# The last two blocks of both output projections join the feed-forward chain as a group

## The chip, the cores and the metric

The kernel runs on one core of a Trainium2 chip. TensorE (PE) multiplies, VectorE (DVE), ScalarE (ACT) and GpSimd (POOL) do the elementwise work, and SyncE (SP) and POOL issue the loads used here. The metric is the device time of one execution in microseconds; lower is better.

## The reference

A decoder trunk of two layers runs over 256 tokens of width 2048 in float32. Each layer normalises, projects, attends (layer A with compressed, selected and windowed keys, layer B with dilated windows; both also to 256 memory tokens), projects back and adds to the residual, and then runs a SwiGLU feed-forward network of inner width 5632. What this case touches is the end of each attention part and the start of each feed-forward network:

```python
o = jnp.concatenate([o_nsa, o_mem], axis=-1) @ w_out      # A: 2048 -> 2048, B: 1024 -> 2048
h = h + o
n = rms_norm(h, norm_ffn)
h = h + (jax.nn.silu(n @ w_gate) * (n @ w_up)) @ w_down   # 2048 -> 5632 -> 2048
```

## The kernel before, in words

**Numbers.** Every float32 operand is split into a high part (a copy in a rounded format, on ACT, L83) and a low part (the rest, a subtraction on DVE, L84). A block product is then three matmuls of 128 x 128 by 128 x 512: high by high, low by high, high by low (`mm3`, L92 to L94, or `hi_lo`, L102, which keeps the third ones for the end of a chunk). Activations stand still in PE, weights stream through. The 256 tokens are two halves of 128.

**Chunks.** `load_w` (L129) loads 512 KB of weights on SP's queue into one of four `raw` buffers and splits them into `whi` and `wlo`, three buffers each. One chunk feeds 12 matmuls.

**Four pairs by seven products.** Gate and up are two 512-wide column blocks, the tokens two halves. For a pair of input blocks (k, k+1) the eight block products of this 2 x 2 by 2 x 2 problem are got from seven products of sums. `Group.steps` has them as s0 to s6: each loads or sums quarters of the weights (1 MB, four pairs at once; tile `q`), splits them into `qhi` and `qlo` (128 x 2048, two buffers each), and does 12 matmuls. s1 and s2 begin with a DVE add on the quarter that the product before has just used; after each of them POOL issues a load that accumulates another quarter onto a used one. s3 uses the first of these, s5 the second. Some results are copied or subtracted between the four PSUM banks of a group. The remaining input blocks of the group are plain chunks (`plain`), one per input block, for all four banks.

The activations for this (`Paired`) are the token halves of each pair and four sums of them, `xhi` and `xlo`: a pair's turn (`turn`, L329) is four PE transposes, two ACT copies into `xf`, a split, four DVE sums of 128 x 128, and a second split. An input block that isn't in a pair has a plain turn: four transposes, two ACT copies and two DVE steps (L86, L87).

**The chain.** `run_groups` goes through the feed-forward groups: eleven gate/up blocks and, after four, four and three of them, two down-projection blocks each. While the chunks of one group run, the seven products of the next one are put between them; `spacing` says how many chunks go ahead of each. Side work (turns) is put in by ticks of three matmuls. The first gate/up block isn't in this form: it is a group of 16 plain chunks (`gu_0`), because nothing before it could carry its seven products. The buffers of the chain (pool `q`) and of its hidden activations (pool `h`) are opened after the pools of the attention part are closed.

**The output projection.** `project_out` works in four blocks of 512 columns. The first two run together as far as attention output is ready (`ready`), then each is finished; after each block the sum is added to the residual `h` (L363), its squares are summed on ACT (L255), and its two turns are put among the next block's matmuls. Blocks three and four are two more calls of `gemm`. Then the norm's factor is made (`finish_rstd`, L245 to L250), and the chain begins.

**Order.** PE's order is as written. The other engines' instructions, SP's loads among them, are ordered by a list scheduler by priority and expected readiness, and then run in that order; `urgent` raises the priority.

## Time and profile before

| what | value |
|---|---|
| median of 3 runs | 2003.47 us (2002.95 to 2003.87) |
| profiled execution | 2003.28 us, its span 2001.5 us |
| PE busy | 1990.3 us, 9315 matmuls, mean granted clock 0.998 |
| DVE busy | 1610.9 us |
| ACT busy | 1241.8 us |
| POOL busy | 66.8 us |
| DMA | 465.75 MB, mean 233 GB/s |

The span goes from the first to the last instruction of the profile. Busy is the time in which an engine worked on an instruction; matmuls are pipelined, so one that lasts 0.39 us still lets the next begin 0.23 us after it. An engine that isn't the bottleneck may stand idle at no cost.

### The profile page before, as it was taken

To read this page: it belongs to the slowest core of one execution; us is meant where nothing else is said; L and a number is where in the kernel's file an instruction comes from. 1 tells how busy PE (TensorE), PEld (TensorE's weight loads), DVE (VectorE), ACT (ScalarE), POOL (GpSimd) and SP (SyncE) were. 2 spreads that over 40 slices of the span, in tenths; PEclk is the share of its full clock that TensorE was granted. 3 is DMA by queue.
4 is the path that set the end of the run, shared out by engine and by line. 5 is a ranking of instruction groups with operands and counts; after the bars stand their busy time and mean duration, and the time that the engine had idled before them with its cause. 6 is when DMAs were issued, how large, how long until landed. Compare 5 with 4: busy or idle time off the path is not lost.

```text
span 2001.5 us, 25392 instructions
## 1 busy us (share of the span) xinstructions
PE 1990.3 (99%) x9315; PEld 1656.8 (83%) x9315; DVE 1610.9 (80%) x2006; ACT 1241.8 (62%) x1561; POOL 66.8 (3%) x96
## 2 busy tenths in 40 slices
PE   9999999999999999999999999999999999999998
PEld 7898888888888888888888888888888888888886
DVE  6767798768888888888887777877888788888886
ACT  7756576656665566656665655656665666655664
POOL 0000000000000000000000000000000000000000
PEclk9999999999999999999999999999999999999999
DMA  9867734587887878878785755497878878788784
GB/s 306 278 204 232 234 113 127 178 261 226 270 285 230 247 238 276 280 229 244 241 273 168 234 168 158 140 304 215 282 240 249 252 257 279 234 243 263 256 257 135
DMA packets 105405, 465.75 MB, mean 233 GB/s; under 512 B 12224, under 2 KB 12608, under 8 KB 83392
## 3 DMA queue, kind: packets, MB, share of 16 engines
q1 hardware_dynamic: 94896, 395.51, 55.2%
q0 software_dynamic: 9952, 67.77, 18.2%
q8 instruction: 73, 1.20, 0.2%
q10 hardware_dynamic: 432, 0.84, 0.1%
q14 instruction: 52, 0.43, 0.1%
HBM read 459.88 MB, written 4.19 MB: 232 GB/s over the span
## 4 chain that ended last, share of the span: by engine, by line
PE 98%; DVE 1%; issue 0%; DMA 0%; ACT 0%; SPq 0%; POOLq 0%; POOL 0%; DVEq 0%; ACTq 0%
PE mm L102 81%; PE mm L93 4%; PE mm L94 4%; PE mm L92 4%; PE aux L344 1%; PE aux L263 1%; PE aux L93 1%; PE aux L94 1%; PE aux L92 1%; PE aux L378 0%; PE cmp L669 0%; PE cmp L668 0%; DMA raw<-in_a_w_mem_kv_dram 0%; DVE xlo L84 0%; DVE wlo L84 0%
## 5 line engine op out<-in xcount | busy, mean ns | idle before, releaser
L84 DVE TENSOR_TENSOR qlo<-q,qhi 128x2048 fp32r<-128x2048 f32 (+1 forms) x224 | 497.9, 2224 | 152.6 <-ACT qhi L83 151.9
L83 ACT ACTIVATE whi<-raw 128x1024 fp32r<-128x1024 f32 (+1 forms) x408 | 424.6, 1043 | 314.6 <-PE mm L102 258.3
L83 ACT ACTIVATE qhi<-q 128x2048 fp32r<-128x2048 f32 (+1 forms) x224 | 417.6, 1865 | 237.5 <-PE mm L102 149.9
L84 DVE TENSOR_TENSOR wlo<-raw,whi 128x1024 fp32r<-128x1024 f32 (+1 forms) x408 | 488.6, 1201 | 94.1 <-ACT whi L83 85.9
L102 PE MATMUL mm<-whi,xhi 128*128 128x512 f32 (+1 forms) x1016 | 391.5, 387 | 0.0
L102 PE MATMUL mm<-whi,xlo 128*128 128x512 f32 (+1 forms) x1016 | 390.8, 386 | 0.0
L102 PE MATMUL mm<-wlo,xhi 128*128 128x512 f32 (+1 forms) x1016 | 273.1, 386 | 0.0
L102 PEld LDWEIGHTS mm<-whi,xlo 128*128 128x128 f32 x1016 | 191.0, 188 | 36.3
L102 PEld LDWEIGHTS mm<-whi,xhi 128*128 128x128 f32 x1016 | 190.9, 188 | 36.3
L102 PE MATMUL mm<-qhi,xhi 128*128 128x512 f32 x560 | 218.7, 391 | 0.0
L102 PE MATMUL mm<-qhi,xlo 128*128 128x512 f32 x560 | 217.9, 389 | 0.0
L102 PEld LDWEIGHTS mm<-wlo,xhi 128*128 128x128 f32 x1016 | 186.7, 188 | 36.4
L87 DVE SCALAR_TENSOR_TENSOR wlo<-raw,gains,whi 128x512 fp32r<-128x512 f32 x160 | 114.5, 747 | 50.7 <-ACT whi L86 46.0
L86 ACT ACTIVATE whi<-raw,gains 128x512 fp32r<-128x512 f32 x160 | 107.8, 717 | 69.8 <-PE mm L102 35.3
L102 PE MATMUL mm<-qlo,xhi 128*128 128x512 f32 x560 | 149.7, 389 | 0.0
L102 PEld LDWEIGHTS mm<-qlo,xhi 128*128 128x128 f32 x560 | 105.1, 188 | 22.0
L102 PEld LDWEIGHTS mm<-qhi,xhi 128*128 128x128 f32 x560 | 105.2, 188 | 21.4
L102 PEld LDWEIGHTS mm<-qhi,xlo 128*128 128x128 f32 x560 | 105.2, 188 | 21.4
L102 PE MATMUL mm<-qhi,hThi 128*128 128x512 f32 x308 | 120.6, 392 | 0.0
L102 PE MATMUL mm<-qhi,hTlo 128*128 128x512 f32 x308 | 119.9, 389 | 0.0
L102 PE MATMUL mm<-whi,hThi 128*128 128x512 f32 x296 | 115.3, 390 | 0.0
L102 PE MATMUL mm<-whi,hTlo 128*128 128x512 f32 x296 | 115.3, 389 | 0.0
(307 smaller groups left out, 2872.5 us busy)
## 6 DMA issues: line engine op xcount, KB each, us to landing
q<-in_a_gu_q_dram SPq DMA_DIRECT2D x40, 1024.0 KB, 6.4
raw<-in_a_gu_s_dram SPq DMA_DIRECT2D x80, 512.0 KB, 7.3
q<-in_b_gu_q_dram SPq DMA_DIRECT2D x40, 1024.0 KB, 6.5
raw<-in_b_gu_s_dram SPq DMA_DIRECT2D x80, 512.0 KB, 7.4
raw<-in_a_dn_s_dram SPq DMA_DIRECT2D x44, 512.0 KB, 6.4
raw<-in_b_dn_s_dram SPq DMA_DIRECT2D x44, 512.0 KB, 6.3
q<-in_a_gu_q_dram POOLq DMA_DIRECT2D x20, 1024.0 KB, 9.8
q<-in_b_gu_q_dram POOLq DMA_DIRECT2D x20, 1024.0 KB, 9.8
```

What stands on the lines that cost most here:

```text
L83: nc.scalar.activation(hi, src, AF.Copy)
L84: nc.vector.tensor_sub(lo, src, hi.bitcast(F32))
L86: nc.scalar.activation(hi, src, AF.Copy, scale=gain)
L87: nc.vector.scalar_tensor_tensor(lo, src, gain, hi.bitcast(F32), op0=ALU.mult, op1=ALU.subtract)
L92: nc.tensor.matmul(o, l[0], r[0], start=start, stop=False, skip_group_check=more)
L93: nc.tensor.matmul(o, l[1], r[0], start=False, stop=False, skip_group_check=more)
L94: nc.tensor.matmul(o, l[0], r[1], start=False, stop=stop, skip_group_check=more)
L102: nc.tensor.matmul(*args, skip_group_check=True, **kw)
L263: nc.tensor.transpose(ps[:, i * P:(i + 1) * P], s, ident)
L344: nc.tensor.transpose(ps[:, i * P:(i + 1) * P], tok[tt][:, i * P:(i + 1) * P], ident)
```

## The change

The third and fourth block of both output projections become one group, `Lead`, at the head of the chain. It has 16 (A) or 8 (B) plain chunks, of which the last three run bank by bank: after each bank's last product DVE adds it to the residual and ACT sums the squares, and after the second and the fourth bank the block's two turns are put into the side work, 4 and 7 ticks later. The seven products of the first gate/up block stand between these chunks by `LEADS`; in layer B only s0 to s4, and s5 and s6 (`own`) go between the next group's first chunks. The first gate/up block takes the form of the others: four pairs by seven products, and eight plain chunks. Side work left at the end of `Lead` is carried on (`leave`).

For this the attention output gets a pool of its own (`po`) that lives until `Lead` is done; pool `q` is opened on the other side of the memory before `Lead` begins, pool `h` after it. Within the chain the pair turns use the three `hb` buffers instead of `xf`. The weights are laid out anew: blocks three and four of `w_out` as chunks of one input block by 1024 columns.

```diff
+TICKS1 = (3, 5)
+LTICKS = (4, 7)
+LEADS = {16: (5, 3, 3, 3, 2, 0, 0), 8: (5, 1, 1, 1, 0)}
...
+        def more(self):
+            self.steps[self.done:] = sorted(self.steps[self.done:] + [(self.now + t, f) for t, f in deferred], key=lambda s: s[0])
+            deferred.clear()
+
+        def leave(self):
+            deferred.extend((t - self.now, f) for t, f in self.steps[self.done:])
+            self.done = len(self.steps)
...
-            f = fpool.tile([P, 1, 4, P], F32, tag="xf", name="xf", bufs=xf_bufs[0])
+            if fpool is fq:
+                f = fq.tile([P, 512], F32, tag="hb", name="xf", bufs=3).rearrange("p (q s t) -> p q s t", q=1, s=4)
+            else:
+                f = fpool.tile([P, 1, 4, P], F32, tag="xf", name="xf", bufs=xf_bufs[0])
...
     def project_out(name, nk, ready, gi):
...
-            residual_block(g[i].ps, i, ssq, op)
-        for nb in range(2, 4):
-            ps = gemm(ob[nb], osx, 512, nk)
-            residual_block(ps, nb, ssq, op, (3, 5) if nb == 2 else (3, 3), nb == 3)
-        return op, finish_rstd(ssq, 4)
+            residual_block(g[i].ps, i, ssq, op, TICKS1 if i else (3, 5), i == 1)
+        return op, ssq
...
+    class Lead(Group):
+        def __init__(self, xs, rest, op, ssq, done):
+            super().__init__(None, None, rest, done)
+            self.xs, self.x_op, self.ssq = xs, op, ssq
+            self.carry = True
+
+        def plain(self, c, side):
+            if c == 0:
+                self.begin()
+            n = len(self.rest)
+            if c < n - 3:
+                ws = load_w(self.rest[c], 512)
+                hi_lo([(self.bank[b], self.xs[c](b % 2), ws[b // 2]) for b in range(4)], side, c == 0)
+            elif c == n - 3:
+                ws = [load_w(self.rest[i], 512) for i in range(c, n)]
+                for b in range(4):
+                    for i, w in enumerate(ws):
+                        mm3(self.bank[b], self.xs[c + i](b % 2), w[b // 2], False, i == 2, True)
+                        side.tick()
+                    nb, tt = 2 + b // 2, b % 2
+                    hb = h[:, tt, nb * 512:(nb + 1) * 512]
+                    nc.vector.tensor_add(hb, self.bank[b], hb)
+                    square_sum(self.ssq[:, tt, nb:nb + 1], hb)
+                    if tt:
+                        deferred.extend(at([urgent(lambda nb=nb, k2=k2: self.x_op.turn(nb, k2, False)) for k2 in range(2)], *LTICKS))
+                        side.more()
...
     def run_groups(groups):
...
+            while own:
+                g.plain(c, side)
+                c += 1
+                own.pop(0)()
             if nxt is not None and nxt.q is not None:
...
-                for ahead, s in zip(spacing(n, nxt.tight), nxt.steps(side)):
-                    for _ in range(ahead):
+                nxt.side = side
+                ss = nxt.steps()
+                spaces = LEADS[n] if g.carry else spacing(n - c, nxt.tight)
+                for ahead, s in zip(spaces, ss):
+                    for _ in range(min(ahead, n - c)):
                         g.plain(c, side)
                         c += 1
                     if c == n and g.done is not None:
-                        side.flush()
+                        if not g.carry:
+                            side.flush()
                         g.done(g)
                         g.done = None
                     s()
+                own = ss[len(spaces):]
...
+        def out_done(g):
+            nonlocal f_r, fh
+            f_r = finish_rstd(ssq, 4)
+            keep.close()
+            fh = phase.enter_context(tc.tile_pool(name="h" + pre, bufs=1))
+
+        wo = a[pre + "_w_out_s"]
+        groups = [Lead(osx, [wo[k] for k in range(wo.shape[0])], op, ssq, out_done)]
...
-                if b == 0:
-                    groups.append(Group(op, None, [a[pre + "_gu_0"][k] for k in range(KT)], done))
-                else:
-                    groups.append(Group(op, [gq[b - 1, i] for i in range(4)], [gs[b - 1, c] for c in range(KT - 2 * NPX)], done))
+                groups.append(Group(op, [gq[b, i] for i in range(4)], [gs[b, c] for c in range(KT - 2 * NPX)], done))
...
     def open_ffn(name):
-        nonlocal fh, fq, fpool, work
+        nonlocal fq, fpool, work
         rota("aux")
-        fh = phase.enter_context(tc.tile_pool(name="h" + name, bufs=1))
-        work = fpool = fq = phase.enter_context(tc.tile_pool(name="q" + name, bufs=1))
+        work = fpool = fq = phase.enter_context(tc.tile_pool(name="q" + name, bufs=1, side="right"))
```

## Rows read from the trace of the kernel before

**Rows 1.** The page's totals and its row of the granted clock in 40 slices.

```profile
PE 1990.3 (99%) x9315; PEld 1656.8 (83%) x9315; DVE 1610.9 (80%) x2006; ACT 1241.8 (62%) x1561; POOL 66.8 (3%) x96
...
PEclk9999999999999999999999999999999999999999
```

**Rows 2.** Waits of PE: engine, line, releaser, us in total, times, longest.

```profile
PE aux L507 <- DVE warm L504: 1.2, 1, 1.2
PE mm L93 <- DVE olo L84: 0.6, 2, 0.3
PE mm L92 <- ACT ohi L83: 0.4, 1, 0.4
```

**Rows 3.** The chain of waits, three stretches: start us, us, what.

```profile
366.68 0.23 PE mm L92
...
415.13 52.38 PE mm L102 x231
...
563.18 0.87 PE aux L344 x8
```

**Rows 4.** Busy by stretch: length, PE, PEld, DVE, ACT, POOL, clock, DMA share, GB/s.

```profile
1281.50:1302.50 21.00, 20.93 (x102) 17.10 (x101) 20.11 (x38) 17.65 (x35) 0.00 (x0) 1.00 0.48 152
...
1374.60:1416.30 41.70, 41.70 (x190) 34.59 (x189) 36.52 (x34) 28.20 (x31) 1.73 (x2) 1.00 0.82 254
```

**Rows 5.** PE in order of time: start us, us, line, operation, tiles.

```profile
1281.19 0.60 PE L329 MATMUL aux<-ident,h 128*128 128x128 f32 x4
1281.54 0.48 PE L92 MATMUL mm<-whi,obhi 128*128 128x512 f32 x1
...
1307.67 1.03 PE L263 MATMUL aux<-ident,h 128*128 128x128 f32 x8
```

**Rows 6.** DVE in order of time, where the old first block began.

```profile
1309.09 0.88 DVE L87 SCALAR_TENSOR_TENSOR xlo<-aux,gains,xhi 128x256 fp32r<-128x256 f32 x2 [0.63 <-ACT xhi L86]
...
1315.19 2.29 DVE L84 TENSOR_TENSOR qlo<-q,qhi 128x2048 fp32r<-128x2048 f32 x1 [3.30 <-ACT qhi L83]
1317.40 2.35 DVE L84 TENSOR_TENSOR wlo<-raw,whi 128x1024 fp32r<-128x1024 f32 x2
```

**Rows 7.** DVE in order of time: the pair turns of layers A and B.

```profile
370.60 0.68 DVE L84 TENSOR_TENSOR xlo<-xf,xhi 128x512 fp32r<-128x512 f32 x1
...
1282.69 0.69 DVE L84 TENSOR_TENSOR xlo<-xf,xhi 128x512 fp32r<-128x512 f32 x1 [0.61 <-ACT xhi L83]
...
1288.13 1.29 DVE L84 TENSOR_TENSOR xlo<-xf,xhi 128x512 fp32r<-128x512 f32 x2
```

**Rows 8.** DVE's groups from 1281.5 to 1302.5: count | busy us, mean ns.

```profile
L84 DVE TENSOR_TENSOR wlo<-raw,whi 128x1024 fp32r<-128x1024 f32 x7 | 8.5, 1214 | 0.0
L84 DVE TENSOR_TENSOR xlo<-xf,xhi 128x512 fp32r<-128x512 f32 x8 | 5.4, 685 | 0.6 <-ACT xhi L83 0.6
...
L87 DVE SCALAR_TENSOR_TENSOR xlo<-aux,gains,xhi 128x256 fp32r<-128x256 f32 x4 | 1.8, 473 | 0.0
L315 DVE TENSOR_TENSOR xf<-xf 128x128 f32<-128x128 f32 x4 | 1.2, 290 | 0.1
```

**Rows 9.** SP's issues in order of time, layer B.

```profile
1293.65 11.22 SPq L129 DMA_DIRECT2D raw<-in_b_gu_dram  x6
1305.82 0.33 SPq L907 DMA_DIRECT2D q<-in_b_gu_q_dram  x1
```

**Rows 10.** PE: the last product that reads layer B's attention output.

```profile
1305.40 0.39 PE L94 MATMUL mm<-wlo,obhi 128*128 128x512 f32 x1
```

**Rows 11.** ACT: the first split of layer B's first quarter.

```profile
1313.24 1.92 ACT L83 ACTIVATE qhi<-q 128x2048 fp32r<-128x2048 f32 x1 [2.76 <-DMA q<-in_b_gu_q_dram]
```

**Rows 12.** Waits of SP's queue: us in total, times, longest.

```profile
SPq L129 <- DVE wlo L84: 1041.6, 374, 8.2
```

**Rows 13.** DMA issues: count, KB each, median us to landing.

```profile
q<-in_b_gu_q_dram SPq DMA_DIRECT2D x40, 1024.0 KB, 6.5
```

**Rows 14.** DVE in order of time: a head's turn in a steady group.

```profile
566.33 1.28 DVE L84 TENSOR_TENSOR hTlo<-aux,hThi 128x512 fp32r<-128x512 f32 x2
```

More of the change, by code (lines that the diff above doesn't have):

```diff
@@ L54, in decoder_trunk @@
     small.tile([P, PADW], F32, name="padw", bufs=1)
+    right = ctx.enter_context(tc.tile_pool(name="right", bufs=1, side="right"))
+    right.tile([P, 64], F32, name="padr")
+    keep = ctx.enter_context(ExitStack())
     phase = ctx.enter_context(ExitStack())
@@ L225, in decoder_trunk @@
     const.tile([P, 32], F32, name="padc")
+    po = keep.enter_context(tc.tile_pool(name="po", bufs=1))
     rota("b3", "aux", "b3")
@@ L500, in o_pair @@
     def o_pair():
-        return pair(lambda i: pa.tile([P, 2, T], F32R, tag=("ohi", "olo")[i], name=("ohi", "olo")[i], bufs=8))
+        return pair(lambda i: po.tile([P, 2, T], F32R, tag=("ohi", "olo")[i], name=("ohi", "olo")[i], bufs=8))
     warm = work.tile([P, 512], BF16, tag="rope2", name="warm")
@@ L924, in keep, with steps @@
             return t
-        def steps(self, side):
+        def steps(self):
             def s0():
@@ L930, in s0 @@
                 self.new(1)
-                self.product(1, 1, self.qa, side, True)
+                self.product(1, 1, self.qa, self.side, True)
                 with tc.high_priority(offset=URGENT):
@@ L938, in s1 @@
                 self.new(2)
-                self.product(2, 7, self.qa, side, True)
+                self.product(2, 7, self.qa, self.side, True)
                 nc.gpsimd.dma_start(self.qb, self.q[2], accum_op=ALU.add)
@@ L945, in s2 @@
                 nc.vector.tensor_add(self.qa, self.qa, self.qc)
-                self.product(1, 5, self.qa, side)
+                self.product(1, 5, self.qa, self.side)
                 nc.gpsimd.dma_start(self.qa, self.q[3], accum_op=ALU.add)
@@ L952, in s3 @@
             def s3():
-                self.product(1, 4, self.qb, side)
+                self.product(1, 4, self.qb, self.side)
                 with tc.high_priority(offset=URGENT):
@@ L959, in s4 @@
             def s4():
-                self.product(2, 6, self.qc, side)
+                self.product(2, 6, self.qc, self.side)
             def s5():
                 self.qb = self.load(3)
-                self.product(1, 3, self.qa, side)
+                self.product(1, 3, self.qa, self.side)
             def s6():
-                self.product(0, 2, self.qb, side)
+                self.product(0, 2, self.qb, self.side)
             return [s0, s1, s2, s3, s4, s5, s6]
@@ L1001, in run_groups @@
             g.buf = ("abc", "cab", "bca")[i % 3]
+        own = []
         for i, g in enumerate(groups):
-            side = take()
+            side = g.side = take()
             n = len(g.rest)
@@ L1021, in run_groups @@
                 c += 1
+            if g.carry:
+                side.leave()
             side.flush()
@@ L1024, in run_groups, with ffn @@
                 g.done(g)
-    def ffn(pre, op, f_r, last):
+    def ffn(pre, op, ssq, last):
         gq, gs = a[pre + "_gu_q"], a[pre + "_gu_s"]
-        groups = []
+        f_r = None
+        def out_done(g):
[5 more added lines that the diff above has]
+        groups = [Lead(osx, [wo[k] for k in range(wo.shape[0])], op, ssq, out_done)]
         for pi, (b0, b1) in enumerate(PORTIONS):
@@ L1080, in __init__, with steps @@
             self.hop = hop
-        def steps(self, side):
+        def steps(self):
             self.op = self.hop()
-            return super().steps(side)
+            return super().steps()
     class Tail(Lazy):
@@ L1128, in decoder_trunk @@
     phase.close()
+    po = keep.enter_context(tc.tile_pool(name="pob", bufs=1))
     rota("b3", "b4", "b3", "aux")
@@ L1164, in ob_slot @@
     def ob_slot():
-        t = pair(lambda i: pc.tile([P, 2, T], F32R, tag=("obhi", "oblo")[i], name=("obhi", "oblo")[i], bufs=4))
+        t = pair(lambda i: po.tile([P, 2, T], F32R, tag=("obhi", "oblo")[i], name=("obhi", "oblo")[i], bufs=4))
         osx.extend(cols((t[0][:, i, :], t[1][:, i, :])) for i in range(2))
@@ L1231, in decoder_trunk @@
     xf_bufs[0] = 3
-    fx, f_r = project_out("b_w_out", 8, 3, 6)
+    fx, f_ssq = project_out("b_w_out", 8, 3, 6)
     stack.close()
     phase.close()
-    open_ffn("fb")
+    open_ffn("b")
     gfin = None
@@ L1355, in _layout @@
     g["a_w_mem_kv"] = _blocks(np, i["a_w_mem_kv"][0])
-    g["a_w_out"] = _blocks(np, i["a_w_out"][0], order=[12, 13, 14, 15] + list(range(12)))
+    for n, order in (("a_w_out", [12, 13, 14, 15] + list(range(12))), ("b_w_out", [0, 4, 1, 5, 2, 6, 3, 7])):
+        w = _blocks(np, i[n][0], order=order, ck=1)
+        g[n] = _blocks(np, i[n][0][:, :1024], order=order)
+        g[n + "_s"] = np.ascontiguousarray(np.concatenate([w[2], w[3]], 2))
     g["w_kv_shared"] = _blocks(np, i["w_kv_shared"])
@@ L1360, in _layout @@
     g["b_w_mem_kv"] = _blocks(np, i["b_w_mem_kv"][0])
-    g["b_w_out"] = _blocks(np, i["b_w_out"][0], order=[0, 4, 1, 5, 2, 6, 3, 7])
     for pre in "ab":
         gate, up, wd = i[pre + "_w_gate"][0], i[pre + "_w_up"][0], i[pre + "_w_down"][0]
-        q, r, first = _pairs(np, gate, up, NFB, NPX)
-        g[pre + "_gu_0"] = first
-        g[pre + "_gu_q"], g[pre + "_gu_s"] = q[1:], r[1:]
+        g[pre + "_gu_q"], g[pre + "_gu_s"] = _pairs(np, gate, up, NFB, NPX)
         for pi, (b0, b1) in enumerate(PORTIONS):
```

18 lines of the change are left out of this document (9 added, 9 removed).

## The prediction

> **What bounds the kernel now.** I read the page's totals first: TensorE (PE) is busy for 1990.3 of the 2001.5 us span, at a granted clock of 9 tenths or more (the top digit) in every slice [rows 1]. A busy PE can still be a PE that waits, so the waits of PE come next: all waits together are 2.2 us, the longest of them 1.2 us and at the start-up multiplication [rows 2]. The chain of waits then gives the price of one product: 231 products in a row take 52.38 us, 226.75 ns each [rows 3]. So the kernel is a queue of products, and time goes only where products go or where a new wait comes. The next limit is VectorE (DVE): in a steady gate/up group it is busy for 36.52 of 41.70 us, ScalarE (ACT) for 28.20; in the middle of layer B's output projection DVE is busy for 20.11 of 21.00 us and PE still does not stop [rows 4]. That stretch is where the change puts new DVE work.
>
> **What is removed.** Per layer the old first gate/up block is 16 chunks of 12 products, 192. The new one is four pairs by seven products (7 x 4 x 3 = 84) and 8 chunks (96), 180. The two output blocks keep their number (192 in layer A, 96 in B), and so do the transposes, 0.87 us for eight [rows 3], 0.44 for four. So 12 products a layer go, 24 in all: 24 x 226.75 ns = 5.44 us. PE does not wait in the old stages, so nothing beyond that can be won; 5.44 is the upper end of the gain.
>
> The Trainium skill ("TensorE: Matmul & The Clock Gate", Back-to-back issue gap) gives about 131 ns per matmul of 512 columns in a stream of weight loads and matmuls, and 216 ns for an isolated one. By the first the removal would be worth 3.1 us at most, by the second 5.2; rows 3 have 226.75 ns, so the trace contradicts the first, and I give it no chance.
>
> **What is added, at no cost.** Per layer seven quarter-sums must be split on ACT and DVE, with two DVE adds and two subtractions, and two accumulating loads come on POOL's queue (2 MB more traffic). Eight chunk splits go. In layer A the new chain step (group Lead) has 276 products, 62.6 us; the DVE work due in it is some 49 us by the durations below, so PE hides it. DMA moves 14.7 MB there (234 GB/s) and 10.5 MB in layer B's 40.8 us (257 GB/s), about the 254 GB/s that a steady group carries without a wait of PE [rows 4]. The moves of pools and the new weight layout change no instruction count. In layer B two of the seven products move into the next group, which has then 6 chunks for the next block's seven: 27.8 us of DVE work in 35.4 us, hidden.
>
> **What is added, at a cost: layer B.** I count from L = 1281.54, the first product after the second block's transposes [rows 5]; it becomes Lead's first. PE's program after L is: five chunks (13.6 us) and two batches of transposes (0.9), so the first quarter-sum product, s0, is due at L+14.5. Then come the last three chunks, s1, s2, s3 and s4 without a chunk between them, with four batches of transposes; s4 ends at L+38.0, and the third of its products that reads the low part begins at L+37.1.
>
> *DVE by that deadline.* Rows overlap by about 0.08 us (2.29 us long, the next 2.21 later [rows 6]), so I count 2.20 for a quarter-sum split or add, 1.13 for a chunk split, 0.6 for a 512-wide step, 0.21 for a 128-wide sum, 0.40 for a 256-wide split [rows 6, 8]. Due: four pair turns, 8 x 0.6 + 16 x 0.21 = 8.2; chunks 3 to 8, 6.8; five splits and two adds, 15.4; two subtractions, 1.2; four residual adds, 2.4; four plain turns, 8 x 0.40 = 3.2; the norm, 0.3. Sum 37.5. The turns begin at 1282.69 [rows 7], L+1.15, so DVE ends at L+38.65 if it never idles: 1.5 us late. If the last turn and the norm slip behind the split, 0.5.
>
> *The first quarter's load.* The new block's buffers lie where the attention's pools lay. In the trace layer B's first quarter is issued 0.4 us after the last product that reads attention output began, and six chunk loads of the same block went ahead of it [rows 9, 10], so I read it as waiting for those pools to be given up. After the change attention output lives elsewhere, and the last use of the old pools is the first block's pair turn: transposed at 1281.19, split on DVE by 1289.4 [rows 5, 7], and perhaps by 1288, since the second block's turn no longer stands between its steps: L+6.5 to L+7.9. From issue to ACT's split took 7.4 us, ACT waiting [rows 9, 11]; then 1.92 for the split: L+15.8 to L+17.2, where PE wants it at L+14.5. With the median landing of 6.5 instead of 7.4 [rows 13] it is L+14.9. PE waits 0.4 to 2.7 us here. This wait and the DVE lateness are the same time seen twice (DVE works on while PE stands), so the larger counts.
>
> *Transposes through one bank.* The last two blocks' transposes go through one PSUM bank, three ticks (9 products, 2.04 us) apart. Where DVE has little to do, two batches end at 1308.70 and the first one's bank is free at 1309.97, 1.7 us after its own batch (0.43 earlier) [rows 5, 6]; in a loaded group it is 3.56 us (564.05 to 567.61) [rows 3, 14]. Three such gaps a layer cost between 0 and 3 x 1.5 = 4.6 us.
>
> I take 1.8 us for layer B (bounds 0.5 and 5: DVE's 1.5, the nearest row being its stretch at 20.11 of 21.00, and a little idleness). In layer A Lead's first product is the one at 366.68 and the first block's turn ends at 371.28 [rows 3, 7]; 7.4 and 1.92 us later, at 13.9 after Lead's start, s0's split is ready, just before 14.5, and DVE has 13 us to spare. Only the bank's gaps count, 0.4 (bounds 0 and 4.6). Waits: 2.2 us. The profiled execution took 2003.28 us for its span of 2001.5, and the median is 2003.47; from the profile 2003.28 - 5.44 + 2.2 = 2000.04, from the median 2000.2, which I predict.
>
> **Rivals.** *All of the gain arrives:* waits under 1.4 us. For: PE's zero waits while DVE was at 96% [rows 2, 4]. Against: the DVE sum above is 0.5 to 1.5 late even without idling. Time: 1998.0 to 1999.4.
>
> *The bank chain in both layers:* each of the six gaps late by 1 us on top of layer B's 1.5: 7.5 us of waits, 2005.5. For: the loaded row's 3.56 [rows 14]. Against: these steps have priority, and DVE is at 78% in layer A's Lead (49 of 62.6 us).
>
> *Slower: the quarter stands behind chunk loads on SP.* SP issues in order, and a chunk load waits there for a free buffer, up to 8.2 us [rows 12]; in the old layer B six chunk loads, the last some 11 us after the first, stood in front of the quarter [rows 9]. From the quarter's landing hangs a serial chain with little to hide it: split 1.92 + 2.2, a chunk split 1.1, add 2.2, split 1.9 + 2.2, add 2.2, split 1.9 + 2.2, the residual adds and turns between, up to 4: 18 to 22 us, due at L+31.3. At a landing of L+13 it is 0 to 4 late. If the quarter is issued at L+11 it lands at L+18.4 and the chain, at 18, is late by 5.1 us: the gain is all but gone. At L+15, one longest wait later than I think, it is late by 9.1, and the kernel is slower: 2003.47 - 5.44 + 9.1 = 2007.1. It decides from an issue later than L+11. Against: the releasing turn is over before most of Lead's chunk loads are due.
>
> *The products are not removed* would show as 9315 matmuls again; the code leaves no way for that.
>
> **How the numbers follow.** A measurement of this kernel can tell about 0.2%, 4.0 us, from no change. The forecast case (waits of 1.4 to 4.5 us, 1999.4 to 2002.5) has 0.47, all of the gain 0.41, the bank chain 0.06, the slower case 0.06. Faster by over 0.2% is below 1999.46: the second case, 0.41. Slower by over 0.2% is above 2007.5: 0.04 of the last cases. The rest, 0.55, is within 0.2%. The range runs from no wait at all, 2003.47 - 5.44 = 1998.0, a tenth less for noise, to 2003.4, which leaves out most of the last two cases and no more.
>
> **What would show it.** 9291 matmuls, and 226.75 ns in the chain as before. Waits of PE at the first quarter-sum product of layer B on ACT's split or the low part on DVE, or at the transposes of the last block; none in steady groups. The quarter's load issued some 6.5 to 8 us after Lead's first product in layer B. DVE without idle time from Lead's first pair turn to s4 in layer B, and idle in layer A. It would be wrong if PE shows no waits there (then DVE did its turns or splits earlier than I place them), or if waits appear in the groups that follow.

## The result: 1% slower, and the profile after

The changed kernel takes 2024.16 us in the median (2023.22 to 2024.94, 4 runs), the kernel before 2003.21; the ratio is 1.0104 (95% interval 1.0087 to 1.0122). I had forecast 2000.2, with 2003.4 as the upper end. The profiled execution took 2024.94 us for a span of 2023.1.

The page's totals and granted clock of the changed kernel (they answer to [rows 1]):

```profile
PE 1994.8 (99%) x9291; PEld 1658.4 (82%) x9291; DVE 1635.6 (81%) x2012; ACT 1255.6 (62%) x1567; POOL 70.9 (4%) x100
...
PEclk9999999999999999999999999989999999999999
```

The 24 products are gone (9291 for 9315), yet PE is busy 4.5 us longer, and one slice of the clock lies below the top digit: that of layer B's `Lead`. Line numbers have moved: L280 transposes of a plain turn, L346 those of a pair turn, L89 and L90 high and low splits, L92 and L93 the same with the gain, L108 products.

The waits of PE (engine, line, releaser, us in total, times, longest; they answer to [rows 2]):

```profile
PE aux L280 <- DVE xlo L93: 9.5, 4, 2.7
PE mm L108 <- ACT qhi L89: 3.8, 2, 3.2
PE aux L280 <- DVE var L262: 2.6, 1, 2.6
PE aux L527 <- DVE warm L524: 1.2, 1, 1.2
```

Only the fourth line was there before. The first and third are the transposes of blocks three and four, 12.1 us (`var` in the third is the norm's sum, which DVE ends 0.07 us after the step that empties the bank); the second is the first quarter-sum product s0, 3.2 us in layer B and 0.6 in A. For all comparisons below I count in the trace the distance between the starts of neighbouring products: what a distance over 0.45 us has beyond 0.227 is a wait. That gives 6.9 us in layer A and 12.9 in layer B, and none anywhere else after the first 10 us; the kernel before has none there.

The rest is the clock. PE in order of time in layer A (start us, us, line, operation, tiles, idle time and its releaser):

```profile
430.16 0.39 PE L108 MATMUL mm<-qlo,xhi 128*128 128x512 f32 x1
433.29 0.63 PE L280 MATMUL aux<-ident,h 128*128 128x128 f32 x4 [2.75 <-DVE xlo L93]
...
434.79 0.63 PE L108 MATMUL mm<-qhi,xhi 128*128 128x512 f32 x1
435.22 0.63 PE L108 MATMUL mm<-qhi,xlo 128*128 128x512 f32 x1
...
437.64 0.40 PE L108 MATMUL mm<-qhi,xlo 128*128 128x512 f32 x1
437.87 0.39 PE L108 MATMUL mm<-qlo,xhi 128*128 128x512 f32 x1
```

After the wait the products start 0.43 us apart until 437.4, then 0.23 again. Busy time by stretch around it (columns as in [rows 4]: behind POOL's come the granted clock, the DMA share and GB/s):

```profile
415.00:440.00 25.00, 19.94 (x82) 15.80 (x81) 14.40 (x19) 15.05 (x23) 0.71 (x1) 0.86 0.54 182
434.10:437.40 3.30, 3.30 (x10) 2.53 (x9) 2.85 (x3) 0.80 (x2) 0.00 (x0) 0.50 0.36 151
438.00:441.40 3.40, 3.40 (x17) 2.80 (x16) 1.33 (x1) 1.91 (x1) 0.00 (x0) 1.00 0.86 296
1288.38:1338.36 49.98, 39.08 (x162) 29.89 (x161) 41.30 (x55) 33.23 (x51) 3.39 (x3) 0.90 0.71 229
```

The second line is wholly at a granted clock of 0.50, the 1.2 GHz level, the third at 1.00, the 2.4 GHz level. In both `Lead`s, and just behind layer B's, 37 products start 0.36 to 0.45 us apart; beyond 0.227 us each they cost 7.3 us. The fourth line runs from layer B's first product in `Lead` (0.09 us after its start) to the end of DVE's split for s4; DVE is idle for 8.7 us of it. The Trainium skill ("TensorE: Matmul & The Clock Gate", "Wait — 56ns, not 53.3ns?") gives 426.7 ns from start to start for 512 columns at the lower level; the rows' 0.43 agree.

So the account closes: -24 x 0.22675 = -5.4 us, waits +19.8, lower clock +7.3, together +21.7. The last product began at 1992.33 before and begins at 2013.99 now, +21.7.

Why the bank is late shows best at the same wait, on ACT and then on DVE (columns as above):

```profile
428.77 0.46 ACT L92 ACTIVATE xhi<-aux,gains 128x256 fp32r<-128x256 f32 x1
429.13 0.59 ACT L994 ACTIVATE mm<-p 128x512 f32<-128x512 f32 x1
430.36 1.91 ACT L89 ACTIVATE qhi<-q 128x2048 fp32r<-128x2048 f32 x1 [0.63 <-PE mm L108]
432.17 0.46 ACT L92 ACTIVATE xhi<-aux,gains 128x256 fp32r<-128x256 f32 x1
```

```profile
428.90 2.29 DVE L90 TENSOR_TENSOR qlo<-q,qhi 128x2048 fp32r<-128x2048 f32 x1
431.11 0.48 DVE L93 SCALAR_TENSOR_TENSOR xlo<-aux,gains,xhi 128x256 fp32r<-128x256 f32 x1
432.66 0.48 DVE L93 SCALAR_TENSOR_TENSOR xlo<-aux,gains,xhi 128x256 fp32r<-128x256 f32 x1 [1.07 <-ACT xhi L92]
```

The bank was filled at 428.4. A turn empties it in two halves, each an ACT copy and a DVE step. Between the halves ACT's fixed order has a copy and a quarter-sum's split, for whose buffer ACT even waits 0.63 us with the second half ready behind it. DVE frees the bank at 433.14, 5.3 us after the batch began at 427.87; the next batch stood 2.04 us of products behind it.

### The profile page after: what moved, and what is told of

Read it like the earlier page. It is cut to its first block, busy times and chain, and to the rows that moved or that the text cites. A ratio compares the mean times of both kernels' runs of the same rounds, so it can differ in the third digit from the quotient of the medians.

```text
span 2023.1 us, 25361 instructions
## 1 busy us (share of the span) xinstructions
PE 1994.8 (99%) x9291; PEld 1658.4 (82%) x9291; DVE 1635.6 (81%) x2012; ACT 1255.6 (62%) x1567; POOL 70.9 (4%) x100
## 4 chain that ended last, share of the span: by engine, by line
PE 97%; DMA 1%; ACT 1%; DVE 1%; issue 0%; SPq 0%; POOLq 0%; POOL 0%; DVEq 0%; ACTq 0%
PE mm L108 80%; PE mm L98 4%; PE mm L99 4%; PE mm L100 4%; PE aux L364 1%; PE aux L280 1%; PE aux L99 1%; PE aux L100 1%; PE aux L98 1%; PE aux L398 0%; ACT qhi L89 0%; PE cmp L689 0%; PE cmp L688 0%; DMA q<-in_a_gu_q_dram 0%; DMA q<-in_b_gu_q_dram 0%
## 5 line engine op out<-in xcount | busy, mean ns | idle before, releaser
L90 DVE TENSOR_TENSOR qlo<-q,qhi 128x2048 fp32r<-128x2048 f32 (+1 forms) x238 | 529.9, 2228 | 153.2 <-ACT qhi L89 151.4
L89 ACT ACTIVATE whi<-raw 128x1024 fp32r<-128x1024 f32 (+1 forms) x392 | 408.2, 1042 | 306.4 <-PE mm L108 253.2
L89 ACT ACTIVATE qhi<-q 128x2048 fp32r<-128x2048 f32 (+1 forms) x238 | 444.1, 1867 | 246.8 <-PE mm L108 150.5
L90 DVE TENSOR_TENSOR wlo<-raw,whi 128x1024 fp32r<-128x1024 f32 (+1 forms) x392 | 469.7, 1201 | 80.1 <-ACT whi L89 74.5
L108 PE MATMUL mm<-whi,xhi 128*128 128x512 f32 (+1 forms) x952 | 367.0, 387 | 0.0
L108 PE MATMUL mm<-whi,xlo 128*128 128x512 f32 (+1 forms) x952 | 366.4, 386 | 0.0
L108 PE MATMUL mm<-wlo,xhi 128*128 128x512 f32 (+1 forms) x952 | 255.7, 386 | 0.0
L108 PE MATMUL mm<-qhi,xhi 128*128 128x512 f32 x616 | 244.5, 397 | 4.5 <-ACT qhi L89 3.8
L108 PE MATMUL mm<-qhi,xlo 128*128 128x512 f32 x616 | 243.9, 396 | 0.0
L108 PEld LDWEIGHTS mm<-whi,xlo 128*128 128x128 f32 x952 | 179.1, 188 | 33.8
L108 PEld LDWEIGHTS mm<-whi,xhi 128*128 128x128 f32 x952 | 179.0, 188 | 33.7
L108 PEld LDWEIGHTS mm<-wlo,xhi 128*128 128x128 f32 x952 | 174.9, 188 | 34.0
L108 PE MATMUL mm<-qlo,xhi 128*128 128x512 f32 x616 | 168.5, 396 | 0.2 <-DVE qlo L90 0.2
L93 DVE SCALAR_TENSOR_TENSOR wlo<-raw,gains,whi 128x512 fp32r<-128x512 f32 x160 | 114.5, 748 | 49.8 <-ACT whi L92 44.4
L92 ACT ACTIVATE whi<-raw,gains 128x512 fp32r<-128x512 f32 x160 | 107.6, 716 | 70.2 <-PE mm L108 30.6
L108 PEld LDWEIGHTS mm<-qhi,xhi 128*128 128x128 f32 x616 | 117.6, 191 | 30.0 <-ACT qhi L89 4.6
L108 PEld LDWEIGHTS mm<-qlo,xhi 128*128 128x128 f32 x616 | 117.1, 191 | 25.6 <-DVE qlo L90 1.2
L108 PEld LDWEIGHTS mm<-qhi,xlo 128*128 128x128 f32 x616 | 117.8, 191 | 24.1
L108 PE MATMUL mm<-qhi,hThi 128*128 128x512 f32 x308 | 120.6, 392 | 0.0
L108 PE MATMUL mm<-qhi,hTlo 128*128 128x512 f32 x308 | 120.1, 390 | 0.0
L108 PE MATMUL mm<-whi,hThi 128*128 128x512 f32 x296 | 115.5, 390 | 0.0
L108 PE MATMUL mm<-whi,hTlo 128*128 128x512 f32 x296 | 115.5, 390 | 0.0
```

Source lines behind the costliest of these rows:

```text
L89: nc.scalar.activation(hi, src, AF.Copy)
L90: nc.vector.tensor_sub(lo, src, hi.bitcast(F32))
L92: nc.scalar.activation(hi, src, AF.Copy, scale=gain)
L93: nc.vector.scalar_tensor_tensor(lo, src, gain, hi.bitcast(F32), op0=ALU.mult, op1=ALU.subtract)
L108: nc.tensor.matmul(*args, skip_group_check=True, **kw)
```

## Experiments

Times are medians; each ratio is against runs of the kernel before on the same chip. "Waits" are counted as above, "clock" is what products 0.36 to 0.45 us apart have beyond 0.227, in the two `Lead`s and just behind them. Waits and clock come from one profiled execution each, which can lie off the median (by +3.6 us in e8, +2.6 in e3, -2.7 in e11), so a difference of a microsecond or two between two rows decides nothing.

| run | us | ratio (95%) | waits A | waits B | clock |
|---|---|---|---|---|---|
| changed kernel | 2024.16 | 1.0104 (1.0087 to 1.0122) | 6.9 | 12.9 | 7.3 |
| e1_two_banks | 2013.61 | 1.0056 (1.0041 to 1.0071) | 3.9 | 11.2 | 2.0 |
| e2_wide_gaps | 2022.70 | 1.0102 (1.0087 to 1.0117) | 4.6 | 14.7 | 5.0 |
| e3_lead_only | 2020.67 | 1.0091 (1.0076 to 1.0106) | 6.1 | 9.0 | 2.9 |
| e4_early_quarter | 2024.60 | 1.0108 (1.0091 to 1.0125) | 6.8 | 13.8 | 5.6 |
| e6_two_banks_later | 2016.27 | 1.0070 (1.0054 to 1.0087) | 1.9 | 13.4 | 2.7 |
| e7_lead_only_two_banks | 2006.46 | 1.0021 (1.0012 to 1.0030) | 1.6 | 1.3 | 0 |
| e8_two_banks_early | 2014.19 | 1.0061 (1.0046 to 1.0076) | 3.2 | 9.3 | 3.8 |
| e9_a_pairs_b_plain | 2004.16 | 1.0010 (1.0001 to 1.0019) | 1.9 | 1.2 | 0 |
| e10_b_no_low | 2009.47 | 1.0037 (1.0023 to 1.0050) | 3.2 | 5.6 | 1.8 |
| e11_b_early_no_low | 2011.24 | 1.0046 (1.0031 to 1.0061) | 3.3 | 7.0 | 0 |
| e12_b_early_later_s4 | 2012.81 | 1.0052 (1.0038 to 1.0065) | 1.9 | 9.8 | 3.3 |
| e13_b_chunks_between | 2013.31 | 1.0051 (1.0036 to 1.0066) | 0 | 12.3 | 3.4 |
| e14_b_between_early | 2009.55 | 1.0031 (1.0020 to 1.0043) | 0 | 10.1 | 2.6 |
| e15_a_pairs_even_turns | 2005.62 | 1.0013 (1.0004 to 1.0022) | 0 | 3.7 | 0 |
| e16_a_only | 2001.51 | 0.9991 (0.9982 to 1.0000) | 0 | 0 | 0 |

### The bank

**e1_two_banks.**

```diff
-                        deferred.extend(at([urgent(lambda nb=nb, k2=k2: self.x_op.turn(nb, k2, False)) for k2 in range(2)], *LTICKS))
+                        deferred.extend(at([urgent(lambda nb=nb, k2=k2: self.x_op.turn(nb, k2, k2 == 1)) for k2 in range(2)], *LTICKS))
```

> Edit: in the last block's turns of Lead the second batch of transposes takes a spare PSUM bank instead of the one bank both share. Theory A (the bank): the waits at transposes, 13 us over both layers, come from a bank that is emptied late, since ScalarE puts a quarter-sum's split between the two halves of the copy; with every second batch in a bank of its own such a wait has two gaps' time to pass, and at most 3 us of the 13 are left. Part of the 7.4 us of products at half the granted clock goes with them. Time 2024.2 - 10 - 4 = 2010, between 2006 and 2014. Theory B (the engines are full): DVE and ACT can't do their work in these stretches; the waits move from the transposes to quarter-sum products, their sum stays at 17 us or more, time 2019 or above. Theory C (the first quarter's load is late) touches nothing here: the 4 to 5 us of waits at s0 stay under A and B alike.

10.5 us faster, inside theory A's 2006 to 2014. Waits of PE in this run:

```profile
PE mm L108 <- ACT qhi L89: 6.1, 3, 4.4
PE mm L108 <- ACT u L941: 2.3, 1, 2.3
PE aux L280 <- DVE xlo L93: 2.2, 1, 2.2
PE mm L108 <- ACT mm L994: 1.4, 1, 1.4
```

Of 12.1 us at the transposes 2.2 are left, as theory A has it. But in layer B theory B is seen too: the sum of waits falls by 1.7 us only, they stand at products now (lines 1, 2 and 4). In the two profiles 4.7 us of waits and 5.3 us of lower clock went.

**e2_wide_gaps.**

```diff
-LTICKS = (4, 7)
+LTICKS = (3, 15)
```

> Edit: the two turns of a block in Lead are put 12 ticks apart and their batches 6 ticks (18 products, 4.08 us) instead of 3 (2.04 us); the bank stays one. Theory A (the bank): waits seen were 2.1 to 3.0 us beyond a gap of 2.04, that is a bank free after 4.1 to 5 us; with gaps of 4.08 at most 1 us is left of each, 3 us over both layers, as many waits as before but none long enough to be followed by half clock: time 2024.2 - 10 - 5 = 2009, between 2005 and 2013; the last turn falls later, so a new wait at s2 to s4 of layer B may take back 1 to 3. Theory B (the engines are full): the same work is due at the same s4, the waits move there and time stays at 2019 or above. Theory C: s0's waits unchanged.

No gain: 1.0102 for 1.0104, a time that theory B had (2019 or above). But most of its waits did not move to s2 to s4, as B has it; 12.5 of 19.3 us stand at transposes. Layer A won 2.3 us of waits, layer B lost 1.8, with one wait of 7.61 us. ACT and PE around it:

```profile
1326.98 0.47 ACT L92 ACTIVATE xhi<-aux,gains 128x256 fp32r<-128x256 f32 x1 [0.55 <-PE aux L280]
1333.89 1.91 ACT L89 ACTIVATE qhi<-q 128x2048 fp32r<-128x2048 f32 x1 [6.44 <-DMA q<-in_b_gu_q_dram]
1335.71 0.46 ACT L92 ACTIVATE xhi<-aux,gains 128x256 fp32r<-128x256 f32 x1
```

```profile
1338.66 1.09 PE L280 MATMUL aux<-ident,h 128*128 128x128 f32 x4 [7.61 <-DVE xlo L93]
```

The second half of a turn stands in ACT's order behind a split that waits 6.44 us for its load. A wider gap doesn't help where the order lets a foreign wait in between the halves: the size of theory A is refuted, its mechanism is seen at its purest.

**e3_lead_only and e7_lead_only_two_banks** have `Lead` and the old first block of 16 plain chunks; e7 gives the second batch the other bank, as e1.

```diff
-                groups.append(Group(op, [gq[b, i] for i in range(4)], [gs[b, c] for c in range(KT - 2 * NPX)], done))
+                if b == 0:
+                    groups.append(Group(op, None, [a[pre + "_gu_0"][k] for k in range(KT)], done))
+                else:
+                    groups.append(Group(op, [gq[b - 1, i] for i in range(4)], [gs[b - 1, c] for c in range(KT - 2 * NPX)], done))
...
```

> Edit: the two output blocks join the chain as group Lead, but gate and up's first block stays 16 plain chunks of 12 products (9315 matmuls); so Lead has no quarter-sum steps in it. Theory A: the transposes wait only because quarter-sum splits stand between the halves of the bank's copy; without them they wait as in the kernel before, and the time is 2003.2 (2002 to 2005), no PE wait over 1 us in Lead. Theory A' (single bank with any split on ACT, quarter-sums or not): three gaps a layer each 1 to 1.5 us late, 2003.2 + 6 to 9 = 2010. Theory B (engines full): 2003.2 as well, since 15 of DVE's 37 us in layer B's Lead go. Theory C: 2003.2.

> Edit: Lead with the first block of gate and up as 16 plain chunks (2020.7 us with one bank), and the second batch of transposes in a bank of its own. Theory A (the bank): the waits at transposes, 14 us over both layers with the half clock behind them, go but for the one on the residual add (1.8): 2020.7 - 12 = 2008 or less, layer B's waits under 3 us. Theory B (the next block's quarter work, which ACT and DVE now do between Lead's steps, fills them): the waits move to products, 2015 or more. If the joining itself cost nothing the time would be 2002.3 to 2003.2, that of the kernel before, and what is left above it (layer A's 3.7 us of waits around 404 to 408, where the last three chunks begin) is a price of Lead that has nothing to do with banks.

All of the theories missed e3, A' by the least: joining the blocks costs 18 us without one product of the seven in `Lead`. The scheduler brings the next block's quarter work forward into these stretches (a quarter's add of 2.28 us on DVE at 1316.42, a split of 1.90 on ACT at 1318.88, between the halves of turns). With the second bank 14.2 of these us go, lower clock among them. PE's waits at the transposes, e3 and then e7:

```profile
PE aux L280 <- DVE xlo L93: 5.9, 4, 2.3
PE aux L280 <- DVE var L262: 2.8, 1, 2.8
PE aux L280 <- DVE h L1033: 1.5, 1, 1.5
```

```profile
PE aux L280 <- DVE h L1033: 0.6, 1, 0.6
...
PE aux L280 <- DVE xlo L93: 0.2, 1, 0.2
```

This pair of runs shows the bank as a cause by itself. 3.9 us above the kernel before are left, 2.9 of them waits.

### Layer B's `Lead`

**e4_early_quarter.**

```diff
-    fpool = pc
-    xf_bufs[0] = 3
+    fpool = po
+    xf_bufs[0] = 2
```

> Edit: in layer B the first block's pair turn takes its two split buffers from the pool that lives on (and only two of them), so the quarter's buffers no longer lie under them, and the first quarter's load need not wait for that turn. Theory C: this wait makes the 3.55 + 0.59 us at s0 of layer B; the load is issued at least 3 us earlier, both waits go, with them the half clock after them (15 products, 3 us at most): time 2024.2 - 4 to 7 = 2017 to 2020. Rival: the load is late because SP had chunk loads in front of it; then its issue moves by under 1 us and the time stays at 2022 to 2026. Theories A and B: the waits at transposes of layer B stay or shift by what s0 no longer gives DVE and ACT: up to 4 us of them may grow back, time up to 2024.

No gain. In the changed kernel the load is issued at 1297.65, 9.4 us after `Lead`'s first product (L = 1288.29), right behind the last step of the first block's pair turns on DVE, and s0 waits (DVE, SP, ACT, PE, one row each of four views):

```profile
1296.89 0.68 DVE L90 TENSOR_TENSOR xlo<-xf,xhi 128x512 fp32r<-128x512 f32 x1
```

```profile
1297.65 1.29 SPq L925 DMA_DIRECT2D q<-in_b_gu_q_dram  x3
```

```profile
1304.35 1.91 ACT L89 ACTIVATE qhi<-q 128x2048 fp32r<-128x2048 f32 x1 [0.49 <-DMA q<-in_b_gu_q_dram]
```

```profile
1306.31 0.50 PE L108 MATMUL mm<-qhi,xhi 128*128 128x512 f32 x1 [3.16 <-ACT qhi L89]
```

With the early load ACT splits the quarter at 1288.07, and s0's wait is gone. In its place stand waits ahead of s0: at a pair turn and at two of `Lead`'s chunks (PE in e4):

```profile
1292.01 0.66 PE L346 MATMUL aux<-ident,h 128*128 128x128 f32 x4 [0.95 <-ACT xf L352]
...
1298.22 0.50 PE L108 MATMUL mm<-whi,obhi 128*128 128x512 f32 x1 [1.66 <-ACT whi L89]
...
1302.64 1.20 PE L108 MATMUL mm<-wlo,obhi 128*128 128x512 f32 x4 [2.31 <-DVE wlo L90]
```

The pair turn's wait may be the price of two buffers for three. The other two wait for chunk splits that now come after the quarter's split on ACT, and its split and add on DVE. Theory C is right on where the wait is from and wrong on what it is worth.

**e6_two_banks_later** (s4 into the next group in layer B), **e8_two_banks_early** (e4 on two banks), **e12_b_early_later_s4** (both). All three also mend layer A, below.

```diff
-LEADS = {16: (5, 3, 3, 3, 2, 0, 0), 8: (5, 1, 1, 1, 0)}
+LEADS = {16: (6, 3, 3, 1, 3, 0, 0), 8: (5, 1, 1, 1)}        # e6, e12
-LTICKS = (4, 7)
+LTICKS = {16: (3, 15), 8: (4, 7)}                           # e6, e8, e12
```

> Edits on top of the two banks (2013.6 us): in layer A the turns of Lead's last block are spread (batches at ticks 3 and 15) and s0 stands one chunk later (6 ahead of it instead of 5); in layer B the fifth product s4 goes into the next group, behind one of its chunks. Layer A, theory A (a place is too early, the engines have time): its waits of 4.8 us with two banks fall under 1.5 and no half clock is left. Theory B (engines full): they stay at 4 or more at other products. Layer B, theory D (too much DVE and ACT work is due in 96 + 60 products): with 12 products more ahead of s4's low part (2.7 us) layer B's waits fall from 11 to 8 or 9; rival E (they come from the late first quarter, 4.8 us, and its consequences): s0's wait stays, the waits behind it sum up as before, 10 to 12. Time: A and D 2013.6 - 4 - 3.4 - 2.5 = 2003.7; A and E 2006; B 2012 or more.

> Edits on top of the two banks (2013.6 us): layer A's last turn spread (batches at ticks 3 and 15), s0 left where it was; layer B with the early first quarter (two pair-turn buffers in the pool that lives on), turns unspread. Layer A, theory A: the wait of 2.6 at the transposes goes with the half clock behind it (3.4), s0's 1.1 us stays: 6 us won. Layer B: theory C (the late quarter alone makes the rest): 11 us of waits fall under 5; theory D (too much work for DVE and ACT ahead of s4): as with one bank the waits at s0 come back at the pair turns and at Lead's chunks, the sum stays at 9 to 12. Time: A and C 2013.6 - 6 - 6 - 3 = 1999; A and D 2007.

> Two banks; layer A with s0 one chunk later and spread turns (waits 1.9 us expected again); layer B with the early first quarter and s4 behind a chunk of the next group. Theory D: the 12 products more ahead of s4 take 2.7 us off layer B's 9.3 us of waits; 6 to 7 left; time 2014.2 - 1.5 - 2.7 = 2010. If the waits lie at Lead's start (pair turns 1.3, chunks 4.3, as with the early quarter before) and not at s4, the sum stays at 9 or more and a new wait stands in the next group, as the 3.7 us on the carried sum's copy did with the late quarter: time 2012 or more.

Layer B's waits: 13.4, 9.3 and 9.8 us for 11.2. A later s4 gives nothing in either form: e6 has more than theory D (8 to 9) or E (10 to 12) wanted, with a new wait of 3.5 us in the next group, at the copy of the carried sum on ACT; e12 keeps 9 or more, as its second branch had it, but with only 0.5 us in the next group. An early quarter takes off 1.9, against theory C. In layer A e6 and e12 are left with 1.9 us; in e8, where s0 stays in its place, 2.2 us stay at a transpose, against theory A. e6 and e8 came out 10 and 7 us above the slowest time forecast with layer A mended (2006 and 2007).

**e10_b_no_low and e11_b_early_no_low** leave 9 us of DVE's work out of layer B's `Lead`, on e1 and on e8.

```diff
-                ws = load_w(self.rest[c], 512)
+                ws = load_w(self.rest[c], 512, low=n > 8)
```

> Two banks (2013.6 us), and in layer B Lead's eight chunks take no low part of the weights: eight DVE instructions of 1.13 us go, 9 us, and the products that read the low part read the high part again (so the low part is left out of these products; their number stays 96). Theory D (the sum of DVE's work due by s4 sets the end): layer B's waits of 11.1 us fall by 6 to 9, to 2 to 5; time 2013.6 - 7 - 2 = 2005. Theory E (the first quarter's late landing and the chain behind it sets it): the wait at s0 stays at 4 to 5, the chain behind it keeps its q adds and splits, the sum stays at 9 or more; time 2012 or more.

> The kernel with two banks and the early first quarter in layer B (2014.2 us), and the low parts of Lead's eight chunks in layer B left out as in the run before this one (the low part is left out of these products). Theory D (sum of work): layer B's waits of 9.3 us fall by 6 or more, to under 3.5; time 2014.2 - 6 - 3 = 2005. Theory E (late landing alone): with the quarter early the waits left are those of the pair turns' two buffers and the turns' banks (1.3 + 2.4 + 1.3), the sum stays at 5 or more. Theory F (both are needed: each of the two is enough to keep PE waiting): waits under 3.5 here, and 6 or more in the run with the late quarter and no low parts.

Layer B's waits are 5.6 us for 11.2 and 7.0 for 9.3. e10 lies near theory D (2 to 5) and not at E (9 or more); e11 is twice D's upper end and fits E (5 or more); F fails in both. But e10 doesn't separate the sum of work from the late quarter: of the 5.6 us that went, 4.0 are s0's wait, and it went because the first quarter came sooner. Its issue on SP and its split on ACT, in e1 and then in e10:

```profile
1292.94 1.28 SPq L925 DMA_DIRECT2D q<-in_b_gu_q_dram  x3
...
1300.87 1.91 ACT L89 ACTIVATE qhi<-q 128x2048 fp32r<-128x2048 f32 x1 [1.72 <-DMA q<-in_b_gu_q_dram]
```

```profile
1289.34 1.28 SPq L928 DMA_DIRECT2D q<-in_b_gu_q_dram  x3
...
1295.20 1.92 ACT L89 ACTIVATE qhi<-q 128x2048 fp32r<-128x2048 f32 x1 [1.15 <-DMA q<-in_b_gu_q_dram]
```

Counted from L (1283.58 in e1, 1281.55 in e10) that is 9.4 and 17.3 us in e1, 7.8 and 13.7 in e10: without the low splits of `Lead`'s chunks between their steps the pair turns, which the load follows, end sooner. From s0's first product to the end of s4's low split it is 26.6 us in e1 and still 25.6 in e10. DVE by form in e1, from L to the end of s4's low split (count | busy us, mean ns | idle before):

```profile
L90 DVE TENSOR_TENSOR qlo<-q,qhi 128x2048 fp32r<-128x2048 f32 x5 | 11.4, 2286 | 1.4 <-ACT qhi L89 1.4
L90 DVE TENSOR_TENSOR wlo<-raw,whi 128x1024 fp32r<-128x1024 f32 x8 | 9.7, 1217 | 0.4 <-ACT whi L89 0.4
L90 DVE TENSOR_TENSOR xlo<-xf,xhi 128x512 fp32r<-128x512 f32 x8 | 5.5, 686 | 1.0 <-ACT xhi L89 1.0
...
L1033 DVE TENSOR_TENSOR h<-mm,h 128x512 f32<-128x512 f32 x4 | 2.7, 687 | 2.0 <-PE mm L100 2.0
```

The stretch from 0.09 us after L to that end in e1, and in e10 (length, PE, PEld, DVE, ACT, POOL, clock, DMA share, GB/s):

```profile
1283.67:1329.39 45.72, 36.99 (x166) 29.33 (x165) 39.99 (x54) 32.81 (x51) 3.45 (x3) 0.96 0.67 208
```

```profile
1281.64:1322.76 41.12, 36.34 (x163) 27.99 (x162) 33.62 (x48) 32.37 (x50) 3.45 (x3) 0.98 0.72 222
```

DVE has 40.0 us to do and stands idle for 5.7, behind ACT's splits, PE's last products and the gaps that its own order leaves: 45.7, where PE wanted the end at 37.1. Without `Lead`'s low splits it has 33.6, idles for 7.5 and ends 4.6 us sooner, 3.6 of them by the earlier quarter. Two chunk splits are left in that stretch, and these must be the next group's, so six of e1's eight are `Lead`'s (DVE by form in e10):

```profile
L90 DVE TENSOR_TENSOR wlo<-raw,whi 128x1024 fp32r<-128x1024 f32 x2 | 2.4, 1218 | 0.0
```

**e13_b_chunks_between and e14_b_between_early** put a chunk between s0, s1, s2 and s3, e14 with the early quarter.

```diff
-            if c < n - 3:
+            u = 3 if n > 8 else 1
+            if c < n - u:
...
-LTICKS = (4, 7)
+LTICKS = {16: ((3, 9), (9, 15)), 8: ((3, 6), (7, 10))}
```

> Two banks; layer B's Lead closes its four sums with its last chunk alone instead of its last three, so that a chunk stands between s0, s1, s2 and s3 (before, s1 to s4 stood without one); layer A with s0 one chunk later and the four batches of transposes 6 ticks apart in banks that alternate. Theory G (neighbouring steps: s3 waits for ACT's copy of s2's sum, s2 for the add behind s1, with no chunk to cover them): of layer B's 11.1 us the 1.2, 1.1 and 2.4 us at s2 to s4 go, s0's 4.8 stays: 5 to 7 us; time 2013.6 - 3 (layer A) - 5 - 1 = 2005. Theory D (sum of DVE's work due by s4): the sum of layer B stays at 9 or more, at s3 and s4 instead; time 2009. Layer A: 1.9 us of waits fall under 1.

> As the run before, and layer B's first quarter is early (two pair-turn buffers in the pool that lives on). Theory G with the late landing as the only other cause: layer B's waits fall under 3; 9291 matmuls, time 2002.4 - 5.4 + 3 + 1 = 2001, a little faster than before. Theory D or F (work has only been moved in front of Lead's chunks): 4 to 5 us of waits at pair turns and at Lead's chunks (1.3, 2.1, 2.7 as with the early quarter before) stay: 2004 to 2007.

Theory G fails: 12.3 and 10.1 us. In e13 a wait of 4.7 us at a transpose takes the place of those at s2 to s4. In e14 5.8 us stay ahead of s0, at a pair turn and at two chunks, where D and F had 4 to 5; 3.9 at two later transposes come on top, and the time is above their 2004 to 2007. Six forms of layer B with the full work of the change (e1, e6, e8, e12, e13, e14) thus have 9.3 to 13.4 us of waits, each at other places.

### Layer A mended, and a version that may win a little

**e9_a_pairs_b_plain, e15_a_pairs_even_turns, e16_a_only.** In layer A s0 stands one chunk later and the four batches of transposes are spread; e15 and e16 have them 6 ticks apart in alternating banks. Layer B has `Lead` with a plain first block in e9 and e15; in e16 it is as in the kernel before.

```diff
+LTICKS = ((3, 9), (9, 15))        # e15, e16; e9: {16: (3, 15), 8: (4, 7)}
+LEADS = {16: (6, 3, 3, 1, 3, 0, 0)}
...
-fx, f_ssq = project_out("b_w_out", 8, 3, 6)
+fx, f_ssq = project_out("b_w_out", 8, 3, 6, True)        # e16: four blocks, as before
```

> Edit: layer A as in the run with s0 one chunk later and spread turns (its waits were 1.9 us, no half clock); layer B with Lead and two banks but the first block of gate and up as 16 plain chunks (its waits were 1.3 us in that form). 9303 matmuls, 12 fewer than before: 2.72 us. If what was read in the two layers separately adds up: 2002.6 - 2.72 + 1.9 + 1.3 = 2003.1, within 0.1% of the kernel before. If the price of the change lies in something common to both layers that the per-layer reading misses: 2006 or more. Under 2001.5 would mean that the waits read are partly not on the path.

> Layer A as in the last two runs (no PE wait over 0.45 us was left in it: s0 one chunk later, the four batches of transposes 6 ticks apart in alternating banks); layer B with Lead, two banks, the batches 6 ticks apart too, and the first block as 16 plain chunks (1.2 us of waits in that form with other ticks). If layer A's 12 products come off in full: 2002.5 - 2.72 + 0 to 1.2 = 1999.8 to 2001.0, faster than the kernel before by 0.07 to 0.14%, which five rounds may just tell apart. Theory of a price outside the waits seen (other stages slower): 2003 or more.

> Layer A with the change and its mended turns (s0 one chunk later, four batches of transposes 6 ticks apart in alternating banks: no PE wait over 0.45 us was left in layer A); layer B's output projection and first block exactly as in the kernel before. 9303 matmuls. If the account by layers holds, no wait is left and the 12 products come off: last product 2.7 us earlier than before, time 2002.6 - 2.7 = 1999.9, a ratio of 0.9986 (0.998 to 0.9995). If the 3.7 us of waits that the run before still had were not layer B's doing but came with layer A's earlier end, they stay: 2003 or more.

e9 came out 1.1 us above the 2003.1 that its waits gave. e15 missed by 4.6 us and more: even turns removed layer A's last wait, but in layer B the waits grew to 3.7 us, 1.5 and 1.0 us of them at a product and a transpose that wait for DVE's residual adds. e16 is 1.4 us faster in the median, as forecast (0.998 to 0.9995), but its interval just reaches 1.0000. PE's waits, and the busy time of layer A's `Lead`, in e16:

```profile
PE aux L527 <- DVE warm L524: 1.2, 1, 1.2
PE mm L99 <- DVE olo L90: 0.3, 1, 0.3
```

```profile
370.00:440.00 70.00, 70.00 (x320) 57.98 (x318) 59.63 (x60) 46.02 (x56) 5.48 (x4) 1.00 0.84 271
```

PE never stops there, with DVE at 59.63 of 70 us. The last product begins at 1988.85, 3.5 us before that of the kernel before: 2.7 are the 12 products, and 0.6 are there already at layer A's first transposes in this stretch (361.56 for 362.18), which the runs don't explain. This execution, 2000.06 us, is one of the two fastest of eleven; in the median only half of the 12 products' 2.7 us shows.

## Why the prediction was wrong, point by point

**Right.** 24 products went, and nothing else of PE's work came; where no wait or clock intervenes the price of 226.75 ns [rows 3] holds. The waits came at the two places named, the first quarter-sum product in layer B and the transposes, and none in the groups that follow. In size all were more: s0's wait in layer B is 3.3 us beyond a product's turn, for 0.4 to 2.7 forecast, and s0 in layer A, which was to be just in time, waits 0.8 us. Layer B's term of 1.8 us measured 12.9, layer A's of 0.4 measured 6.9.

**The step that failed most: "Transposes through one bank", taken at 0.4 us in layer A and at nothing in layer B's 1.8.** Measured at transposes, by starts: 5.4 us in layer A (2.5 + 2.9) and 7.8 in layer B (2.1 + 2.7 + 3.0), 13.2 in all with the bounds at 4.6 a layer. I took the 3.56 us of a turn in a loaded group [rows 14] for the upper end, but a turn in `Lead` has two halves on two engines with instructions of 1.9 and 2.3 us between them, and the bank of the example took 5.3. Against my own words, priority did not keep them together. That layer A has DVE time to spare is true and didn't help: ACT stood idle before a split while the second half waited behind it. e3 against e7 shows it: one bank or two, 14 us. The rival with the bank chain in both layers, 2005.5, had the mechanism, with 7.5 us of waits for the 19.8 measured.

**"DVE ends at L+38.65 if it never idles."** In the changed kernel DVE stood idle for 8.7 us up to that end. In e1, free of the one bank, it ended at L+45.8. Of the 7 us, 2.3 are two chunk splits of the next group that the order puts ahead of that end (`Lead`'s six I had), and the idle time is 5.7, where my sum has only the 1.15 before its start. That e10 has half of e1's waits doesn't show DVE's sum to be the price: most of what went there is s0's wait.

**"The first quarter's load"** was issued at L+9.4, not L+6.5 to L+7.9, and ACT took it up 6.7 us later, at L+16.1. What it follows was read rightly: the pair turns end on DVE at 1297.57. But three low splits of `Lead`'s chunks, 1.22 us each, stand between their steps; without them, in e10, the issue is at L+7.8. Its worth was misread too: the serial chain that the slower rival counts, 18 to 22 us due at L+31.3, makes 0.6 to 6.0 us at the forecast landing (L+13.9 to L+15.3) and 2.8 to 6.8 at the measured one, where the forecast took 1.8. Nor does an early load alone mend it: e4 and e8 took s0's wait away and got back 0 and 1.9 us of layer B's waits. The slower rival, the quarter behind chunk loads on SP, did not happen: it decides from L+11.

**A wait was priced at its own length.** 37 products at or near the 1.2 GHz level's 0.43 us cost 7.3 us more; no term of mine had them. In e1 they fall with the waits, to 2.0 us.

**What stays open.** In layer B with two banks the waits move and keep a sum of 9 to 13 us. Less DVE work takes it down, mostly by way of an earlier quarter; an early load with all of the work hardly does. How much of the rest is the fixed order on ACT and DVE, how much their sum and how much the chain behind the quarter, no run separates. An order written by hand that keeps a turn's halves together was not tried.

## What to carry to other kernels

A PSUM bank that is emptied in several steps on two in-order engines is free only after the foreign instructions, and the foreign waits, that their order puts between those steps (5.3 us in the example, and in e2 a split alone waited 6.44); when work is moved to where long splits run, give it a second bank before counting its gaps. Where an engine comes out at 101% of the time to a deadline in a sum made without idling, price its idle time from a loaded stretch, and count the late case as the forecast. Price a wait of TensorE with the products at half clock that may follow it.

## What the runs showed of the hardware that was not expected

Waits of PE of 2.1 us or more (beyond a product's turn) were often followed by a stretch at a granted clock of 0.50, products 0.43 us apart: 3.4 or 6.8 us long, in e2 once 10.2 around the end of its wait of 7.8. It began during the wait or at most 1.6 us after its end. Not each was: in the changed kernel those of 2.5 and 2.9 us in layer A and of 3.3 in layer B were, one of 2.1 in layer B was not; in e1 one of 2.4 in layer A was and one of 2.4 in layer B was not. In layer A of e3 such a stretch came behind two waits of 1.3 and 0.7 us. The kernel before and e16 have no such stretch between start-up and the end.
